# Expert weights loaded in 1 MB units with 8 KB rows, inputs gathered by every fourth column, and an overflow branch written as loops

## The chip, the core and the metric

One core of one Trainium2 chip. TensorE (PE) multiplies, VectorE (DVE), ScalarE (ACT) and GpSimd (POOL) do the rest, and SyncE (SP) issues all DMAs from one queue. The metric is the device time of one launch in microseconds (us). The kernel before took 753.24, 752.36 and 753.23 us in three runs, median 753.23 us.

## The reference

Two layers on 256 tokens of width 1024, all in float32. Each layer has a mixer (layer 0: sparse attention, layer 1: latent attention) beside a cross-attention, one output projection, a residual with layer norm, and a mixture of experts:

```
hdn = silu(einsum('sd,edf->sef', xs, w_gate)) * einsum('sd,edf->sef', xs, w_up)
hdn = hdn * gate[..., None]          # gate: top-1 group of 4, top-2 experts within it
f   = einsum('sef,efd->sd', hdn, w_down)
x   = layer_norm(ALPHA * x + f, ln_g, ln_b)
```

There are 16 experts of hidden width 512. Each of the three matrices of an expert is 1024 x 512 floats, 2 MB, so that the experts of a layer hold about 100 MB, and the two layers read nearly all of their bytes for them.

## The kernel before, in words

**The mixture of experts.** `moe` (L1459) works through eight pairs of experts, k = 0 to 7. Up to 64 tokens are taken for each expert. For a pair, `gather` (L1521, pairs 0 and 1) or `gather_two` (L1508, two pairs at once) multiplies the tokens x_tm, as the stationary operand, by a 0/1 matrix of the chosen tokens. The result is the pair's input, transposed: eight chunks of 128 model columns by 128 places. A layer has five such gathers of 32 matmul instructions each (a float32 matmul shows as two instructions): two for the pairs 0 and 1, one each for the pairs 2 and 3, 4 and 5, 6 and 7. `up` (L1553) then multiplies the chunks by the gate weights and again by the up weights, the result is transposed in four blocks (L1682), multiplied by the down weights (L1728, for the last pair L1749), and `combine` (L1567) adds it back to the tokens. All of it is in program order on PE.

**Chunks.** A unit of gate or up weights is 256 rows of a matrix, two to a partition: partition p holds the rows 2p and 2p+1, 4 KB that are contiguous in memory. So the c-th chunk of inputs must hold every second model column (`chunk`, L1484), and PE loads its stationary operand from x_tm with a step of two floats. In the first gather of a layer the gains of the layer norm are applied chunk by chunk, from a small tile `vcol2` that is laid out in the same way; it comes from `vwide`, transposed in `g_pe` (L1038).

**Loads.** `plan_pair` (L278) lists the units of a pair: 24 units of 512 KB. `pump` (L228) goes through one list of all loads of the kernel in order; each takes a free slot in an arena of the on-chip memory, or in spare rooms that are opened during the experts, and is issued on SP's queue. When there is no slot, it stops until `drop` has freed one. SP waits for the last reader of a slot, and for earlier loads: some eight are under way at a time. `up` waits for the two units of a step, multiplies two chunks, frees both units and pumps. The inputs of the pairs stand in two more slots of the arena, xg0 and xg1 (`grab`, L1477).

**The overflow branch.** An expert may have been chosen by more than 64 tokens. Then the rest is computed by `overflow` (L1579), at the end of each layer, with all experts by all tokens. It stands under `tc.If(flag > 0)` (L1591), and its body is unrolled: 16 experts by 4 blocks of the hidden width, with 16 float32 matmuls for gate, 16 for up and 4 for down in each. With the inputs given the branch isn't taken, and every engine jumps over its part of the body. After it come the layer norm of layer 0 and the latent attention (`mla`, L1802: statistics L836, norm L877 and L878, 12 matmuls that only keep PE busy, L472, transposes L903), or in layer 1 `finish` (L2003), which writes the output.

## Time and profile before

| what | us |
|---|---|
| median of three runs (752.36 to 753.24) | 753.23 |
| the execution that was profiled | 753.32 |
| its span, first to last instruction | 751.5 |

| engine | busy us | share of the span |
|---|---|---|
| PE, matmuls | 706.3 | 94% |
| PE, loads of stationary operands | 416.9 | 55% |
| DVE | 310.1 | 41% |
| ACT | 194.4 | 26% |
| POOL | 146.4 | 19% |

235.67 MB went through the DMA queues, a mean of 314 GB/s. PE's busy time counts matmuls as they are in the pipeline, with ends that are modelled, so it hides short waits. The experts of layer 0 run from about 199 to 418 us and those of layer 1 from about 525 to 737 us.

### The profile page before, as it was taken

What the parts mean: (1) busy time and instruction counts of PE and PEld (TensorE: products, weight loads), DVE (VectorE), ACT (ScalarE), POOL (GpSimd) and SP (SyncE); (2) the same over time, 40 slices, a digit from 0 to 9 for tenths busy, and PEclk for the clock granted to TensorE, in tenths of its full rate; (3) what the DMA queues carried; (4) which work ended last, traced back from release to release, by engine and by line L of the source; (5) the groups of instructions that cost most, each with busy time, mean ns of one, the idle gap of its engine ahead of it and who ended that gap; (6) DMA issues with size and microseconds to landing.
All of it is one profiled execution on the core that took longest, in us unless ns stands there. A gap on an engine that the chain in (4) does not pass through costs nothing. (4 is left out here: it accounts for less than half of the span.)

```text
span 751.5 us, 11046 instructions
## 1 busy us (share of the span) xinstructions
PE 706.3 (94%) x4119; PEld 416.9 (55%) x4119; DVE 310.1 (41%) x732; ACT 194.4 (26%) x478; POOL 146.4 (19%) x165
## 2 busy tenths in 40 slices
PE   6999989889999999999999699999999999999992
PEld 6988978667643535335324377777444435343341
DVE  3389588994641211121110547747412212121105
ACT  3342253553320211101101265543212001011010
POOL 6876536030210400000000252021302000000002
PEclk9999999998999999999999899999999999999996
DMA  9876673935788999999999896457989999999981
GB/s 306 251 223 180 214 282 119 346 92 168 282 334 320 408 345 408 410 408 408 408 410 377 301 386 211 160 197 270 346 320 409 409 408 410 409 409 408 410 322 59
DMA packets 88625, 235.67 MB, mean 314 GB/s; under 512 B 13356, under 2 KB 32879, under 8 KB 88559
## 3 DMA queue, kind: packets, MB, share of 16 engines
q1 hardware_dynamic: 88558, 234.83, 83.5%
q8 instruction: 36, 0.59, 0.3%
q14 instruction: 31, 0.25, 0.1%
HBM read 233.76 MB, written 1.05 MB: 312 GB/s over the span
## 5 line engine op out<-in xcount | busy, mean ns | idle before, releaser
L369 POOL TENSOR_TENSOR wl<-arena,wh 128x1024 fp32r<-128x1024 f32 (+3 forms) x36 | 83.2, 2334 | 35.8 <-PE s L643 10.4
L1673 DVE SCALAR_TENSOR_TENSOR arena<-arena,u 128x512 f32<-128x512 f32 x16 | 12.0, 748 | 186.5 <-PE u L1559 105.4
L1559 PE MATMUL u<-arena 128*64 128x512 f32 x332 | 82.6, 594 | 0.8 <-DMA arena<-in_moe_w_up_dram 0.7
L871 POOL TENSOR_TENSOR lnmv<-lnmv,mhalf 128x1 f32<-128x1 f32 x8 | 6.4, 801 | 378.0 <-DVE lnmv L870 377.7
L1559 PE MATMUL g<-arena 128*64 128x512 f32 x324 | 79.5, 594 | 0.2 <-DMA arena<-in_moe_w_gate_dram 0.2
L1728 PE MATMUL yb<-arena 128*64 128x512 f32 x316 | 76.6, 595 | 0.0
L1733 DVE TENSOR_TENSOR y<-yb,y 128x512 fp32r<-128x512 f32 x28 | 19.4, 692 | 85.7 <-ACT y L1732 85.3
L1559 PEld LDWEIGHTS u<-arena 128*64 128x64 f32 x332 | 26.0, 137 | 48.8 <-issue 42.0
L660 ACT ACTIVATE arena<-s,mx 128x128 f32<-128x128 f32 (+1 forms) x88 | 37.4, 435 | 55.5 <-DVE mx L654 53.0
L1559 PEld LDWEIGHTS g<-arena 128*64 128x64 f32 x324 | 24.8, 137 | 43.7 <-issue 40.4
L1728 PEld LDWEIGHTS yb<-arena 128*64 128x64 f32 x316 | 23.7, 137 | 39.8 <-issue 37.9
L1732 ACT CAST y<-yb 128x512 fp32r<-128x512 f32 x28 | 16.4, 585 | 94.2 <-PE yb L1728 94.2
L1570 PE MATMUL acc<-y,SkT 128*128 128x512 f32 (+1 forms) x136 | 38.6, 406 | 0.0
L1684 ACT COPY arena<-hT 128x256 f32<-128x256 f32 x16 | 6.0, 372 | 119.3 <-DVE arena L1684 119.3
L1671 ACT ACTIVATE arena<-g 128x512 f32<-128x512 f32 x16 | 9.6, 597 | 93.4 <-PE g L1559 93.3
L1559 PE MATMUL g<-split,arena 128*64 128x512 f32 x104 | 32.3, 592 | 0.2 <-DMA split<-in_moe_w_gate_dram 0.2
L1570 PEld LDWEIGHTS acc<-y,SkT 128*128 128x128 f32 x136 | 22.5, 188 | 15.9 <-issue 12.9
L1728 PE MATMUL yb<-split,arena 128*64 128x512 f32 x116 | 31.1, 596 | 0.0
L654 DVE TENSOR_REDUCE mx<-s 128x1 f32<-128x128 f32 (+1 forms) x88 | 27.0, 362 | 4.9 <-PE s L643 3.3
L1559 PE MATMUL u<-split,arena 128*64 128x512 f32 x100 | 28.6, 592 | 0.0
L683 PE MATMUL pT<-ident,arena 128*128 128x128 f32 x140 | 22.4, 290 | 4.5 <-DVE arena L673 2.1
L673 DVE TENSOR_SCALAR arena<-arena,sm 128x128 f32<-128x128 f32 (+1 forms) x48 | 26.2, 588 | 0.9
(409 smaller groups left out, 1283.5 us busy)
## 6 DMA issues: line engine op xcount, KB each, us to landing
arena<-in_moe_w_gate_dram SPq DMA_DIRECT2D x97, 512.0 KB, 10.2
arena<-in_moe_w_down_dram SPq DMA_DIRECT2D x93, 512.0 KB, 10.2
arena<-in_moe_w_up_dram SPq DMA_DIRECT2D x92, 512.0 KB, 10.2
split<-in_moe_w_down_dram SPq DMA_DIRECT2D x31, 512.0 KB, 10.2
split<-in_moe_w_gate_dram SPq DMA_DIRECT2D x26, 512.0 KB, 10.2
split<-in_moe_w_up_dram SPq DMA_DIRECT2D x25, 512.0 KB, 10.2
arena<-in_nsa_w_in_dram SPq DMA_DIRECT2D x7, 1024.0 KB, 7.5
arena<-in_w_out_dram SPq DMA_DIRECT2D x8, 512.0 KB, 11.9
```

Of the source, the lines that this page charges most:

```text
L369: lo[j].tensor_tensor(wl[:, c, :], t[:, c, :], wh[:, c, :].bitcast(F32), op=OP.subtract)
L654: V.tensor_reduce(self.mx[i][:, t:t + 1], v, axis=AX.X, op=OP.max, negate=True)
L660: SC.activation(self.p[i][:, a:a + n], self.sb[i][:, a:a + n], AF.Exp, bias=self.mx[i][:, t:t + 1], scale=1.0, accum_out=self.sm[i][:, t:t ...
L673: V.tensor_scalar(v, v, self.sm[i][:, t:t + 1], g, op0=OP.mult, op1=OP.mult)
L683: PE.transpose(pt[:, j * P:(j + 1) * P], self.p[i][:, a:a + P], ident)
L1559: PE.matmul(b_[e * 64:(e + 1) * 64, :], at[k][1](i * 2 + c)[:, e * 64:(e + 1) * 64], w_[e][:, c, :], start=(i + c == 0), stop=(i == 3 and ...
L1570: PE.matmul(acc[t][hf][:, a:b], SkT[k % 2][:, t * P:(t + 1) * P], yhl[hf][n][:, a:b], start=(k == 0 and n == 0), stop=(k == 7 and n == 1 a ...
L1671: SC.activation(h_sb, gp, AF.Silu)
L1673: V.scalar_tensor_tensor(h_sb, h_sb, gs[:, k % 2:k % 2 + 1], up_, op0=OP.mult, op1=OP.mult)
L1728: PE.matmul(yb[hf][e * 64:(e + 1) * 64, :], hT[:, c, e * 64:(e + 1) * 64], w_[e][:, 0, hf * 512:(hf + 1) * 512], start=(c == 0), stop=(c = ...
L1732: SC.copy(yhl[hf][0], yb[hf])
L1733: V.tensor_tensor(yhl[hf][1], yb[hf], yhl[hf][0].bitcast(F32), op=OP.subtract)
```

## The change

Five things change together.

1. Units of 1 MB: a unit of gate or up weights is now 512 rows, four to a partition (8 KB contiguous), one of down weights 256 rows of 1024, two to a partition (8 KB). A pair has 12 units. The down units of the last pair stay as they were. Slots are taken at multiples of 8 KB, or of 4 KB for what is at most 4 KB.
2. `chunk` takes every fourth column, so that PE's stationary operand is read with a step of four floats (16 bytes). `vwide`, `vcol2` and the transposes in `g_pe` follow. The four transposes of the hidden values read every second column, except in the last pair.
3. xg0 is allocated with the temporaries of the layer, xg1 beside the split of x; the one-unit room `slot` goes; the limits of the arena are 12.25 and 8.25 KB in place of 12.5, 8.5 and 8.5, 4.5 KB.
4. Two small tiles (`sv`, `gs`) move into a constant tile.
5. The body of the overflow branch has two loops on the chip, over 16 experts and 4 blocks, in place of 64 copies.

```
-            return slice(m // 2 * 256 + m % 2, (m // 2 + 1) * 256, 2)
+            return slice(m // 4 * 512 + m % 4, (m // 4 + 1) * 512, 4)
...
+        for nm, w in (("g", A["moe_w_gate"]), ("u", A["moe_w_up"])):
+            for q in range(2):
+                for e in range(2):
+                    plan("%s%d_%d_%d_%d" % (nm, l, k, q, e), [P, 4, FF],
+                         (None, w[l, 2 * k + e][q * 512:(q + 1) * 512, :].rearrange("(p c) f -> p c f", c=4)))
+        w = A["moe_w_down"]
+        if k < 7:
+            for q in range(2):
+                for e in range(2):
+                    plan("d%d_%d_%d_%d" % (l, k, q, e), [P, 2, D],
+                         (None, w[l, 2 * k + e][q * 256:(q + 1) * 256, :].rearrange("(p c) f -> p c f", c=2)))
+            return
...
         def up(k, nm, b_):
-            for i in range(4):
-                keys = ["%s%d_%d_%d_%d_%d" % (nm, l, k, i // 2, i % 2, e) for e in range(2)]
+            for i in range(2):
+                keys = ["%s%d_%d_%d_%d" % (nm, l, k, i, e) for e in range(2)]
                 w_ = [get(key) for key in keys]
-                for c in range(2):
+                for c in range(4):
                     for e in range(2):
-                        PE.matmul(b_[e * 64:(e + 1) * 64, :], at[k][1](i * 2 + c)[:, e * 64:(e + 1) * 64], w_[e][:, c, :],
-                                  start=(i + c == 0), stop=(i == 3 and c == 1))
+                        PE.matmul(b_[e * 64:(e + 1) * 64, :], at[k][1](i * 4 + c)[:, e * 64:(e + 1) * 64], w_[e][:, c, :],
+                                  start=(i + c == 0), stop=(i == 1 and c == 3))
...
-                for e in range(NE):
-                    for f in range(FF // P):
-                        fs = slice(f * P, (f + 1) * P)
+                with tc.For_i(0, NE, 1) as e:
+                    with tc.For_i(0, FF // P, 1) as f:
...
-                                V.scalar_tensor_tensor(z, yo, go[:, t, e:e + 1], z, op0=OP.mult, op1=OP.add)
+                                V.scalar_tensor_tensor(z, yo, go[:, t, 0:1], z, op0=OP.mult, op1=OP.add)
...
-                PE.transpose(b_[:, j * P:(j + 1) * P], h_sb[:, j * P:(j + 1) * P], ident)
+                PE.transpose(b_[:, j * P:(j + 1) * P], h_sb[:, j * P:(j + 1) * P] if k == 7 else
+                             h_sb[:, j // 2 * S + j % 2:(j // 2 + 1) * S:2], ident)
```

## Rows read from the trace of the kernel before

**Rows 1.** Stretches: length, busy PE, PEld, DVE, ACT, POOL, clock, DMA share, GB/s.
```profile
300.00:350.00 50.00, 50.00 (x247) 20.73 (x247) 8.56 (x17) 5.45 (x10) 0.00 (x0) 1.00 1.03 409
...
720.20:724.90 4.70, 4.70 (x25) 2.71 (x23) 1.17 (x2) 0.37 (x1) 0.00 (x0) 1.00 1.05 377
```

**Rows 2.** Timeline of PE, layer 0, pairs 6 and 7: start, length, instruction, count.
```profile
358.95 0.59 PE L1559 MATMUL g<-slot,arena 128*64 128x512 f32 x1
...
372.79 1.21 PE L1570 MATMUL acc<-y,SkT 128*128 128x512 f32 x4
...
382.44 2.74 PE L1559 MATMUL g<-split,arena 128*64 128x512 f32 x10
...
402.18 1.22 PE L1570 MATMUL acc<-y,SkT 128*128 128x512 f32 x4
```

**Rows 3.** Timeline of PE, layer 1, the last pair's gate, and the combine after its up.
```profile
708.38 2.31 PE L1559 MATMUL g<-arena 128*64 128x512 f32 x9
...
722.22 1.20 PE L1570 MATMUL acc<-y,SkT 128*128 128x512 f32 x4
```

**Rows 4.** Timeline of PE, the first gather, and the ends of a gather for two.
```profile
199.56 4.07 PE L1526 MATMUL xg<-arena,x_tm 128*128 128x128 f32 x32
...
297.06 0.28 PE L1515 MATMUL xg<-SkR,xh 128*128 128x256 f32 x1
...
300.78 0.28 PE L1515 MATMUL xg<-SkR,xl 128*128 128x256 f32 x1
```

**Rows 5.** Groups of PE's loads by form: count, busy us, mean ns, idle before.
```profile
L1515 PEld LDWEIGHTS xg<-SkR,xh 128*128 128x128 f32 x96 | 18.7, 195 | 1.8 <-ACT y L1732 1.6
L1526 PEld LDWEIGHTS xg<-arena,x_tm 128*128 128x128 f32 x128 | 15.6, 196 | 2.3 <-issue 1.6 <-DVE arena L1490 0.7
L1559 PEld LDWEIGHTS u<-arena 128*64 128x64 f32 x332 | 26.0, 137 | 48.8 <-issue 42.0 <-DMA arena<-in_moe_w_up_dram 5.9 <-DMA arena<-in_moe_w_down_dram 0.9
L1836 PEld LDWEIGHTS mi<-arena 128*128 128x128 f32 x16 | 2.9, 189 | 2.7 <-issue 1.9 <-ACT arena L1822 0.8
```

**Rows 6.** Groups of VectorE's reductions by form, same columns.
```profile
L654 DVE TENSOR_REDUCE mx<-s 128x1 f32<-128x256 f32 x52 | 20.6, 415 | 1.5 <-PE s L638 1.5
L654 DVE TENSOR_REDUCE mx<-s 128x1 f32<-128x128 f32 x36 | 10.3, 285 | 3.4 <-PE s L643 3.3
L848 DVE TENSOR_REDUCE arena<-arena 128x20 f32<-128x160 f32 x2 | 0.8, 421 | 0.0
L1401 DVE TENSOR_REDUCE y<-y 128x40 f32<-128x160 f32 x2 | 0.6, 320 | 0.1
```

**Rows 7.** Line 1591: sequencer instructions; ns min/median/max, first and last start.
```profile
L1591 ACTq COMPARE_BRANCH  x2: 45/48/50, 416.8 to 736.2; - x2
L1591 ACTq EVENT_SEMAPHORE  x2: 17/17/17, 417.2 to 736.6; - x2
L1591 DVEq COMPARE_BRANCH  x2: 63/68/72, 417.3 to 736.6; - x2
L1591 PEldq COMPARE_BRANCH  x2: 3386/4712/6037, 417.7 to 737.1; - x2
L1591 DVEq EVENT_SEMAPHORE  x2: 21/21/21, 423.1 to 739.5; - x2
```

**Rows 8.** Timeline around the branch, layer 0, then layer 1.
```profile
423.28 0.70 DVE L836 BATCH_NORM_STATS2 lnst<-acc 128x6 f32<-128x512 f32 x1 [5.62 <-DVEq L1591]
423.91 5.28 PE L472 MATMUL warm<-onesb 128*128 128x512 bf16 x12 [6.29 <-PEq L1591]
...
425.55 0.75 DVE L878 SCALAR_TENSOR_TENSOR x_tm<-x_tm,lnmv,arena 128x512 f32<-128x512 f32 x1 [0.46 <-POOL lnmv L871]
...
428.98 0.66 PE L903 MATMUL pt<-ident,x_tm 128*128 128x128 f32 x4
429.48 1.03 PE L472 MATMUL warm<-onesb 128*128 128x512 bf16 x4
...
739.65 0.70 DVE L836 BATCH_NORM_STATS2 lnst<-acc 128x6 f32<-128x512 f32 x1 [2.41 <-DVEq L1591]
```

## The prediction

> **What bounds the kernel now.** The first view is the table of stretches. In the middle of an expert stage PE is busy all of the time at full clock and the DMAs run at 409 GB/s [rows 1]; the two are nearly balanced, so the table can't say which of them sets the end. The timeline of PE can. In layer 0, pair 6 goes from its first gate matmul at 358.95 to its first combine at 372.79, in 13.84 us; pair 7 needs 19.74, from 382.44 to 402.18 [rows 2]. The 5.90 us between them are waits for weights: the groups of PE's loads put 5.9 us of idle time on up weights [rows 5]. So layer 0 becomes bound by the DMAs in its last pair and by PE before. In layer 1 the last pair takes 13.84 us again (708.38 to 722.22) [rows 3]: PE sets the pace to the end, and whatever is added to PE there is added to the time. The third view is the one line of the branch. In layer 0 PE's jump takes 6.04 us, VectorE's next instruction comes 5.8 us after its own compare, and in layer 1 it is 3.39 and 2.9 us [rows 7]; the normalization starts after it [rows 8].

> **Gathers by every fourth column: the term that decides.** A gather's PE time is now set by 32 instructions at 0.120 us ((300.78 - 297.06) / 31), 3.84 us [rows 4]. Its matmuls take some 0.107 us of that, an estimate for 256 columns from warming matmuls of 512, four of which take 1.03 us with the tail of the last, so some 0.21 each [rows 8]. The load of the stationary operand is hidden behind them as long as it is the shorter one. What does the load take? Contiguous, 64 columns show 137 ns and 128 columns 189, so 0.81 ns per column and 85 fixed; with a step of two floats the 128 columns show 195 and 196 [rows 5]. So a step of 8 bytes costs 6 ns, and no row has PE reading with a step of 16. The lower bound is that it costs as little again: pace 0.12, nothing. The upper bound comes from VectorE, which does read one float in 20. Its contiguous reductions take 285 ns for 128 elements and 415 for 256, 1.02 ns per element and 155 fixed, which gives 318 for 160 elements where 320 is shown; with a step of 80 bytes the same 160 take 421, or 1.66 ns each [rows 6]. If each newly fetched group of bytes takes 1.66 ns on PE too, the small rise at 8 bytes says how large the group is: with groups of 16 bytes the 128 columns are 64 fetches, 106 ns against 104 for the columns themselves, just over the edge; with 8 bytes it would be 212, which isn't seen, and with 32 bytes there would be no rise. At a step of 16 bytes each column is then a fetch: 128 x 1.66 = 212 ns, twice the matmul. I take this end, since it alone explains the rise, though the step of 8 bytes is the nearer row. The pace becomes 212 and a few ns, 0.22 us; a gather 7.04; five gathers of a layer cost 5 x 3.2 = 16.0 us more on PE. Between the two ends lies a load that adds VectorE's extra 0.64 ns to each column, 186 ns: pace 0.19, 11.2 us per layer.

> [...]

> In layer 1 the 16.0 us are on the path. In layer 0 they come before the last pair, whose waits of 5.90 they swallow: the weights land meanwhile. Layer 0 pays 16.0 - 5.9 = 10.1.

> **Larger units.** Two bounds from the stretches: rows of 4 KB at 409 GB/s are 160.2 ns on each of 16 engines; where rows of 2 KB flow, at 377, 86.9 [rows 1]. A row's fixed part is then 2 x 86.9 - 160.2 = 13.6 ns; an 8 KB row takes 306.8 and the rate is 427, 4.4% more. The other end is no gain, since a stretch that short may be poor in DMAs for another reason. Either way it is worth nothing where PE bounds. A step of `up` now waits for two units of 1 MB and then multiplies four chunks; the part that follows the last landing is two chunks longer, 2 x 13.84 / 16 = 1.7 us, which counts only where weights are late. SP issues half as many loads; PE's waits halve, hidden.

> **The branch.** ACT's body before is 64 activations, and its next instruction follows the compare by 0.4 us; VectorE's, with five vector operations in each of 64 copies, stalls 5.8, and PE's, with thousands, 6.0 [rows 7]. Short bodies are jumped without a stall. In loops, VectorE's body is some 25 operations and PE's some 180 records (16 transposes, 36 matmuls), the one below ACT's, the other between ACT's and VectorE's. I take both as free. In layer 0 VectorE's statistics then start 5.4 us earlier, and the first norm, which ends at 426.30, at 420.9. PE, now idle 6.29 us and then at half clock for 12 warming matmuls (5.28 us, where later four take 1.03), would do them in some 2.7 and be done at 420.9 also; the transposes, at 428.98 today, start at 421.2 [rows 8]: 7.8 us gained, and the attention behind them follows, its weights having been issued before the branch. In layer 1 only VectorE matters: it idles 2.41 us, of which 2.3 go [rows 8]. If PE's jump stays, layer 0 gains nothing, since its warming ends last already. The loops' own costs lie in the body that isn't run; if they put a barrier on the path beside it, that is at most the present stall again.

> **The rest.** Four more transposes at the start, and the limits of the arena, are hidden: 14 slots of 8 KB against 28 of 4 KB. The transposes of the hidden values read every second float: between nothing and the 6 ns that this step costs a gather's load [rows 5], 4 x 14 of them cost at most 0.3, which I take.

> **Sum, likeliest.** +10.1 (layer 0, gathers less waits) - 7.8 (its branch) + 16.0 (layer 1, gathers) - 2.3 (its branch) + 0.3 = +16.3. The profiled execution took 753.32, its span 751.5 and 1.8 around it; 753.3 + 16.3 = 769.6. The median of the runs is 753.23, 0.1 from the profiled one, so 769.6 stands for it too. With the load at 186 ns it is 753.3 + 5.3 - 7.8 + 11.2 - 2.3 + 0.3 = 760.0; the case's own range is 758 to 774.

> **Rival 1: every fourth column is free.** For it: the step of 8 bytes costs 6 ns, and VectorE needn't tell of PE. Then layer 0's waits shrink: 100 us of loads ahead of the last pair at 4.2% less are 4.2 us, less 1.7 for the longer last step, 2.5 gained. Layer 1 gains its branch alone. 753.3 - 2.5 - 7.8 - 2.3 + 0.3 = 741.0; 739 to 747, by the DMAs' rate. It decides if the load stays under 0.107.

> **Rival 2: PE's load slows by half of it** (a load of 145 to 165 ns). Layer 0 even, layer 1 +6: 753.3 + 0.5 - 7.8 + 6 - 2.3 + 0.3 = 750.0.

> **Rival 3: PE still stalls at the jump**, since its body lies between the two known lengths; layer 0's 7.8 are not gained. 777.4 with slow loads, 748.8 with free ones. [...]

> **Chances.** Likeliest case 0.48, rival 1 0.38, rival 2 0.07, rival 3 0.07. About 0.2% is what a measurement of this kernel can tell from no change. Slower: 0.48, and 0.05 of rivals 2 and 3, 0.53; same 0.04; faster 0.38 and 0.05, 0.43. Cases of both signs hold most of it, so the range has to span them: 740 leaves out a fifth of rival 1, 773 what of the stalls lies above.

> **What would show it.** The stationary loads of the gathers at 295 ns (85 + 212) where 195 stood, 0.22 us from one to the next and a gather of 7 us; the last pair of layer 0 in 13.8 us with no wait for weights; the compare on PE and VectorE under 0.1 us, and the statistics 0.4 us after it. Loads at 200 ns make the prediction wrong at its main term, and the time is then near 741.

## The result and the profile after

The changed kernel takes 773.0 us, median of four runs (772.74 to 774.40), against 753.24 before: a ratio of 1.0269 [1.0251, 1.0287], 19.8 us slower. That is the likeliest case of the prediction, but 3.4 us above its 769.6, and just above the upper end, 773, of its range: the two middle runs took 772.79 and 773.22. The profiled execution has a span of 771.1 us, 19.6 more than before, and the stretches below add up to that.

The groups of PE's stationary loads by form, of the changed kernel, answer to [rows 5] (count, busy us, mean ns, idle before):

```profile
L1513 PEld LDWEIGHTS xg<-SkR,xh 128*128 128x128 f32 x96 | 31.6, 329 | 1.8 <-ACT y L1733 1.6
L1524 PEld LDWEIGHTS xg<-arena,x_tm 128*128 128x128 f32 x128 | 30.3, 328 | 2.3 <-issue 1.6 <-DVE arena L1487 0.7
L1557 PEld LDWEIGHTS u<-arena 128*64 128x64 f32 x176 | 15.8, 137 | 25.1 <-issue 25.1
L1681 PEld LDWEIGHTS hT<-ident,arena 128*128 128x128 f32 x64 | 8.8, 202 | 3.3 <-DVE arena L1672 3.3
```

The loads of the gathers take 329 ns where 195 stood, and up's loads in this row no longer wait for weights. The timeline of PE shows the first gather, a gather for two pairs from its first to its last matmul, the last pair of layer 0 from gate to combine, and that of layer 1 ([rows 2 to 4] of before):

```profile
198.04 7.73 PE L1524 MATMUL xg<-arena,x_tm 128*128 128x128 f32 x32
...
306.81 0.28 PE L1513 MATMUL xg<-SkR,xh 128*128 128x256 f32 x1
...
313.93 0.39 PE L1513 MATMUL xg<-SkR,xl 128*128 128x256 f32 x1
...
399.46 0.59 PE L1557 MATMUL g<-split,arena 128*64 128x512 f32 x1
...
413.30 1.20 PE L1566 MATMUL acc<-y,SkT 128*128 128x512 f32 x4
...
730.76 3.60 PE L1557 MATMUL g<-arena 128*64 128x512 f32 x16
...
744.60 1.21 PE L1566 MATMUL acc<-y,SkT 128*128 128x512 f32 x4
```

From one gather matmul to the next it is now (313.93 - 306.81) / 31 = 0.230 us, where 0.120 stood. Both last pairs take 13.84 us, layer 0's too: its weights have landed while PE was held up in the gathers. The sequencers at the branch (now line 1587), and the timeline behind it in layer 0 and layer 1 ([rows 7, 8] of before):

```profile
L1587 DVEq COMPARE_BRANCH  x2: 56/64/72, 428.4 to 759.0; - x2
L1587 DVEq EVENT_SEMAPHORE  x2: 21/21/21, 428.8 to 759.7; - x2
L1587 PEldq COMPARE_BRANCH  x2: 318/338/358, 428.8 to 759.5; - x2
```

```profile
429.33 2.75 PE L475 MATMUL warm<-onesb 128*128 128x512 bf16 x12 [0.61 <-PEq L1587]
429.35 0.70 DVE L839 BATCH_NORM_STATS2 lnst<-acc 128x6 f32<-128x512 f32 x1 [0.58 <-PEq L1587]
...
432.52 0.63 PE L906 MATMUL pt<-ident,x_tm 128*128 128x128 f32 x4 [0.44 <-DVE x_tm L881]
...
759.85 0.70 DVE L839 BATCH_NORM_STATS2 lnst<-acc 128x6 f32<-128x512 f32 x1 [0.21 <-DVEq L1587]
```

PE's jump fell from 6.0 and 3.4 us to 0.36 and 0.32, VectorE's next instructions come 0.4 and 0.7 us after its compare, the 12 warming matmuls take 2.75 us where 5.28 stood (granted clock 1.00 in place of 0.50), and the transposes now wait for VectorE's norm, by 0.44 us.

Taking the same marks in both traces, the 19.6 us are: -1.5 before the first gather, +18.5 from it to the last pair of layer 0 (182.88 to 201.42), -5.9 in that pair, -7.6 at its branch (transposes 3.54 later, where the combine was 11.12 later), +0.1 to layer 1's first gather, +18.7 to its last pair (182.81 to 201.51), 0.0 in it, and -2.8 from the last matmul to the end.

The first of these isn't the change's. The table of stretches of the kernel before, and then of the changed one (length, busy PE, PEld, DVE, ACT, POOL, clock, DMA share, GB/s):

```profile
60.00:64.00 4.00, 4.00 (x22) 3.97 (x22) 3.43 (x12) 3.32 (x10) 0.00 (x0) 0.57 0.91 268
```

```profile
60.00:64.00 4.00, 4.00 (x35) 4.00 (x35) 3.43 (x12) 3.35 (x10) 0.00 (x0) 1.00 0.85 264
```

In both executions PE had been idle for most of the 2 us before (busy 0.69 and 0.73 us from 58 to 60); from 60 to 64 its granted clock was 0.57 in the one execution and 1.00 in the other. The lower clock comes and goes between executions: from 60 to 62 two kernels below were granted 0.50 (the units alone) and 1.00 (the loops alone), and another, profiled twice, starts its first gather at 199.40 and at 198.01.

### The profile page after: what moved, and what is told of

It reads as the page before. It is cut to its first block, busy times and chain, and to the rows that moved or that the text cites. A ratio compares the mean times of both kernels' runs of the same rounds, so it can differ in the third digit from the quotient of the medians.

```text
span 771.1 us, 10672 instructions
## 1 busy us (share of the span) xinstructions
PE 735.7 (95%) x4123; PEld 452.3 (59%) x4123; DVE 310.9 (40%) x732; ACT 194.5 (25%) x478; POOL 146.8 (19%) x165
## 5 line engine op out<-in xcount | busy, mean ns | idle before, releaser
L1729 PE MATMUL yb<-arena 128*64 128x512 f32 x328 | 85.3, 595 | 0.0
L1672 DVE SCALAR_TENSOR_TENSOR arena<-arena,csb,u 128x512 f32<-128x512 f32 x16 | 12.0, 747 | 180.9 <-PE u L1557 99.7
L1557 PE MATMUL g<-arena 128*64 128x512 f32 x200 | 53.8, 593 | 0.0
L1557 PE MATMUL u<-arena 128*64 128x512 f32 x176 | 50.4, 592 | 0.0
L1557 PE MATMUL u<-arena,xg 128*64 128x512 f32 x168 | 39.6, 592 | 0.0
L1557 PE MATMUL g<-arena,xg 128*64 128x512 f32 x144 | 39.6, 592 | 0.0
L1513 PE MATMUL xg<-SkR,xl 128*128 128x256 f32 x96 | 38.0, 396 | 0.0
L1513 PE MATMUL xg<-SkR,xh 128*128 128x256 f32 x96 | 37.8, 394 | 0.0
L1513 PEld LDWEIGHTS xg<-SkR,xh 128*128 128x128 f32 x96 | 31.6, 329 | 1.8 <-ACT y L1733 1.6
L1566 PEld LDWEIGHTS acc<-y,SkT 128*128 128x128 f32 x136 | 22.6, 189 | 15.9 <-issue 12.9
L1524 PEld LDWEIGHTS xg<-arena,x_tm 128*128 128x128 f32 x128 | 30.3, 328 | 2.3 <-issue 1.6
## 6 DMA issues: line engine op xcount, KB each, us to landing
split<-in_moe_w_gate_dram SPq DMA_DIRECT2D x13, 1024.0 KB, 12.5
```

The costliest lines, as they stand in the source:

```text
L1513: PE.matmul(b_[:, c * S:(c + 1) * S], v[:, t, chunk(2 * c0 + c)], SkR[:, t].rearrange("p e s -> p (e s)"), start=(c == 0 and t == 0 and v ...
L1524: PE.matmul(b_[:, c * P:(c + 1) * P], x_tm[:, t, chunk(c0 + c)], Sk[:, t].rearrange("p e s -> p (e s)"), start=(t == 0), stop=(t == 1))
L1557: PE.matmul(b_[e * 64:(e + 1) * 64, :], at[k][1](i * 4 + c)[:, e * 64:(e + 1) * 64], w_[e][:, c, :], start=(i + c == 0), stop=(i == 1 and ...
L1566: PE.matmul(acc[t][hf][:, a:b], SkT[k % 2][:, t * P:(t + 1) * P], yhl[hf][n][:, a:b], start=(k == 0 and n == 0), stop=(k == 7 and n == 1 a ...
L1672: V.scalar_tensor_tensor(h_sb, h_sb, gs[:, k % 2:k % 2 + 1], up_, op0=OP.mult, op1=OP.mult)
L1729: PE.matmul(yb[hf][e * 64:(e + 1) * 64, :], hT[:, 2 * q + c, e * 64:(e + 1) * 64], w_[e][:, c, hf * 512:(hf + 1) * 512], start=(q + c == 0 ...
```

## The experiments

**The two parts alone.** The first kernel keeps units and gathers of before and takes the loops; the second is the changed kernel with the branch unrolled again.

```diff
-                for e in range(NE):
-                    for f in range(FF // P):
+                with tc.For_i(0, NE, 1) as e:
+                    with tc.For_i(0, FF // P, 1) as f:
```

> The kernel before, with the body of the overflow branch alone written as loops on the chip; units and gathers stay as they were. Theory A (the two parts of the change are separate, the branch gives back what the trace shows): the jump costs PE some 0.35 us in place of 6.0 and 3.4, the first transposes of layer 0's normalization start 7.6 us earlier and VectorE's last statistics 2.2 us earlier, so 753.2 - 9.8 = 743.4 us, and all of it stays. Rival C (the earlier start is lost again, since layer 1's attention or experts then wait for weights that arrive no earlier): the stretch from the branch to the last pair of layer 1 grows by what the branch gave, 749 to 753 us. In both the gathers keep 0.12 us from one matmul to the next and the last pair of layer 0 its 5.9 us of waits.

> The changed kernel with the body of the branch unrolled again as before: the larger units and the gathers by every fourth column alone. Theory A: 773.0 + 9.8 = 782.8 us, PE's jump back at about 6 and 3.4 us. Rival C: the branch was worth little in the total and the units cost less than the gathers show, 773 to 777 us.

The loops alone: 742.80 against 751.96 of the kernel before on the same chip, ratio 0.9874 [0.9851, 0.9897], 9.2 us faster. The units alone: 784.75 (782.8 expected), ratio 1.0436 [1.0411, 1.0461], 32.8 us slower. The product of the two, 1.0305, is 0.4% above the 1.0269 of the whole change, no more than the intervals allow, so neither part needs the other. Theory A holds, and rival C falls: from the transposes behind the branch to layer 1's first gather the loops alone take 96.54 us and the kernel before 96.59, so what the branch gave isn't lost there. A little of it is lost later: layer 1's last pair now waits for weights and takes 14.29 us from gate to combine in place of 13.84. PE's jump in the units alone:

```profile
L1587 PEldq COMPARE_BRANCH  x2: 3326/4752/6177, 430.3 to 769.1; - x2
```

**Step or size.** One index of the changed kernel, and then one rearrangement of its weights (with the index of the gathers and the layout of the gains, which follow it):

```diff
-            return slice(m // 4 * 512 + m % 4, (m // 4 + 1) * 512, 4)
+            return slice(m * P, (m + 1) * P)
```

> The changed kernel with one index changed: the gathers read 128 neighbouring columns in place of every fourth (which leaves out the matching of the columns with the rows of the weights, so the values differ); units, transfers, waits and the number of instructions stay. Theory A (the step of 16 bytes alone makes the stationary load slow): loads of 189 ns, a gather of 3.7 us, and 753.2 - 9.8 for the branch, less 0.8 for layer 1's gathers without a step and 0 to 2.5 for the shorter waits in layer 0's last pair: 740 to 742.6 us. Rival B (the loads are slow because transfers of 8 KB rows write the on-chip memory beside them): loads stay near 329 ns and the time near 773 us.

```diff
-plan(..., [P, 4, FF], (None, w[...][q * 512:(q + 1) * 512, :].rearrange("(p c) f -> p c f", c=4)))
+plan(..., [P, 2, 2 * FF], (None, w[...][q * 512:(q + 1) * 512, :].rearrange("(b p c) f -> p b (c f)", b=2, c=2)))
-            return slice(m // 4 * 512 + m % 4, (m // 4 + 1) * 512, 4)
+            return slice(m // 2 * 256 + m % 2, (m // 2 + 1) * 256, 2)
```

> The changed kernel with the gate and up units still of 1 MB, but each as two rows of 4 KB per partition, so that the gathers read every second column again; the down units keep their 8 KB and the branch its loops. The result is the reference's. Theory A: gathers at 0.12 us again, and 1 MB units are worth nothing where PE bounds; layer 0's last pair waits about 5.9 us and up to 1.7 more for its longer last step: 743 to 745 us. Rival B (the size of the units is what slows the loads or the stages): over 755 us. If 8 KB rows of the down weights alone make the transfers faster, the waits of layer 0 fall and it is 741 to 743 us.

With neighbouring columns: 739.04, ratio 0.9823 [0.9801, 0.9846], 12.9 us faster than before. With 1 MB units and steps of two floats: 744.11, ratio 0.9897 [0.9877, 0.9917], and loads of 196 ns. The first one's loads, the same loads of the second, and the first one's rate in mid-stage:

```profile
L1513 PEld LDWEIGHTS xg<-SkR,xh 128*128 128x128 f32 x96 | 18.4, 191 | 1.8 <-ACT y L1733 1.6
L1557 PEld LDWEIGHTS u<-arena,xg 128*64 128x64 f32 x168 | 12.7, 137 | 24.7 <-issue 22.3 <-DMA arena<-in_moe_w_up_dram 2.4
```

```profile
L1513 PEld LDWEIGHTS xg<-SkR,xh 128*128 128x128 f32 x96 | 18.8, 196 | 1.8 <-ACT y L1733 1.6
```

```profile
300.00:350.00 50.00, 50.00 (x247) 20.96 (x244) 8.82 (x18) 5.26 (x10) 0.00 (x0) 1.00 1.01 419
```

In the first one the transfers of 8 KB rows and the instructions are the same, and the loads are back at 191 ns: the step alone makes them slow, and rival B falls. With PE that much faster, up waits for weights again (2.4 us in the row). This is the world of the prediction's first rival, and its 741.0 was near. The expectation's 740 to 742.6 was counted from 753.2 and is 1 us too high, about as much as the kernel before took less on this chip (751.96). The 8 KB rows give 419 GB/s where 409 stood [rows 1], and the waits of layer 0's last pair shrink: 17.04 us from gate to combine, 19.74 before.

**The price of a step.** Sets of 24 equal matmuls behind the end of the kernel before, one line each:

```diff
+    [PE.matmul(bb[:, 0:256], xa[:, 0:382:3], mv, start=True, stop=True) for _ in range(24)]
```

> The kernel before, with sets of 24 matmuls behind its end, which differ in one thing each: the step with which the stationary operand of 128 columns is read (1, 2, 3, 4, 6, 8, 12, 15 floats; 1, 2, 4, 6, 8, 16 values of 2 bytes), with 64 moving columns or 256; and, with a contiguous stationary operand, the step of 256 moving columns (1, 2, 3, 4, 7 floats). Only the rows of these sets count, not the time. Theory A (the load pays for each group of 16 bytes that it touches, 0.2335 us / 128 = 1.82 ns): 32, 64, 96, 128 groups at steps 1 to 4 and 128 beyond, so a load-bound pace of 0.107 at step 1 and 0.117, 0.175, 0.234 us at 2, 3, 4, and 0.234 at all larger steps; values of 2 bytes slow down by the step in bytes, 0.117 at 4 (8 bytes), 0.175 at 6 (12), 0.234 at 8 (16). Rival D (a threshold: every step of 16 bytes or more costs a column 1.82 ns, below it nothing): step 3 like step 2, about 0.107 to 0.117. Rival E (the cost grows with the step itself): step 8 near 0.47 us. Moving columns, if they are read in the same way: 256 of them 0.11 us at step 1, 0.35 at step 3, 0.47 at step 4 and 7.

The loads of the sets with 256 moving columns, at a granted clock of 1.00: steps of 1, 2, 3, 4 and 8 floats (ns min/median/max, first and last start):

```profile
L2057 PEld LDWEIGHTS bench<-SkR,xh x24: 188/192/224, 797.6 to 800.4; 128*128 128x128 f32 x24
L2058 PEld LDWEIGHTS bench<-SkR,xh x24: 195/195/198, 800.5 to 803.3; 128*128 128x128 f32 x24
L2059 PEld LDWEIGHTS bench<-SkR,xh x24: 251/261/261, 803.4 to 807.4; 128*128 128x128 f32 x24
L2060 PEld LDWEIGHTS bench<-SkR,xh x24: 317/329/332, 807.5 to 812.9; 128*128 128x128 f32 x24
L2061 PEld LDWEIGHTS bench<-SkR,xh x24: 337/337/341, 813.1 to 818.7; 128*128 128x128 f32 x24
```

From load to load that is 0.12, 0.12, 0.174, 0.235 and 0.243 us. Step 3 touches 96 groups of 16 bytes and step 4 128; 0.174 / 96 and 0.235 / 128 are both 1.8 ns. Rival D (step 3 like step 2) and rival E (step 8 twice step 4) fall: at steps of 3 and 4 these paces fit a load that pays 1.8 ns for each group of 16 bytes that it touches. The sets with 64 moving columns show the same in another light, since PE, which had a granted clock of 1.00 until 751 (the set of step 1), had 0.50 from 753 to 792. Steps 1, 3, 4, 6 and 12, and the table of a stretch of step 4:

```profile
L2043 PEld LDWEIGHTS bench<-SkR,xh x24: 190/192/192, 748.8 to 751.5; 128*128 128x128 f32 x24
L2045 PEld LDWEIGHTS bench<-SkR,xh x24: 329/329/331, 756.4 to 761.3; 128*128 128x128 f32 x24
L2046 PEld LDWEIGHTS bench<-SkR,xh x24: 329/329/331, 761.5 to 766.9; 128*128 128x128 f32 x24
L2047 PEld LDWEIGHTS bench<-SkR,xh x24: 316/318/319, 767.1 to 772.2; 128*128 128x128 f32 x24
L2049 PEld LDWEIGHTS bench<-SkR,xh x24: 364/369/369, 778.2 to 784.3; 128*128 128x128 f32 x24
```

```profile
761.60:766.90 5.30, 5.30 (x24) 5.30 (x25) 0.00 (x0) 0.00 (x0) 0.00 (x0) 0.50 0.00 0
```

At 1.00 the contiguous loads follow one another at (751.5 - 748.8) / 23 = 0.117 us. At 0.50 step 3 rises from 0.174 to (761.3 - 756.4) / 23 = 0.213 us, but step 4 takes the same 0.235 as at 1.00: its price did not rise with the lower clock. Beyond step 4 theory A's one price is only near: at 0.50 it is 0.222 us at step 6, 0.239 at 8, 0.265 at 12 and 0.230 at 15, so 1.7 to 2.1 ns a column. What sets these differences isn't shown. Its figures for moving columns and for values of 2 bytes were wrong; the last section has them.

**How long a body is jumped without a stall.** The kernel before, with 4, 8, 1 and 2 experts written out in the body of a loop:

```diff
+                with tc.For_i(0, NE // 4, 1) as eo:
+                    for j in range(4):
+                      for f in range(FF // P):
```

> The kernel before, with a middle length of the overflow branch: a loop over four groups of 4 experts, and inside it 4 experts written out. PE's body has 592 matmuls, 1184 records with their loads, where the loops have 52 matmuls and the full body 2320. [...] Rival G (the stall grows with the length that is jumped): a quarter of 6.0 and 3.4, so 1.5 and 0.9 us, and some 2 us in the time.

> The same with two groups of 8 experts: PE's body has 1168 matmuls, 2336 records. [...] Rival G: half, 3 and 1.7 us, 747. [...]

> The kernel before, with the overflow branch as one loop over the 16 experts whose four column blocks are written out: PE's body has 160 matmuls, 320 records with their loads; VectorE's some 35 operations. The runs so far show PE's jump at 0.34 us over 52 matmuls and at 3.3 to 6.1 us over 592, 1168 and 2320 alike, so the stall is no price per instruction but one that sets in between 104 and 1184 records. If it sets in above 320: compare 0.35 us and a time near 743. If below: 3.3 and 6.1 us and 749 to 751.

> The same with two experts written out: PE's body has 304 matmuls, 608 records. If the stall sets in above 608: 0.35 us and a time near 743. If below: 3.3 and 6.1 us and 749 to 751. A stall between the two (half of it) would speak for a price by length after all.

One execution each: 749.58, 753.38, 750.63 and 751.18 us, with 752.64 (the first two) and 751.44 (the others) for the kernel before beside them. PE's jump, with 1 and with 4 experts written out:

```profile
L1591 PEldq COMPARE_BRANCH  x2: 3426/4762/6097, 417.4 to 736.9; - x2
```

```profile
L1591 DVEq COMPARE_BRANCH  x2: 63/68/72, 416.8 to 735.8; - x2
L1591 PEldq COMPARE_BRANCH  x2: 3346/4712/6077, 417.2 to 736.3; - x2
L1591 DVEq EVENT_SEMAPHORE  x2: 21/21/21, 417.4 to 736.5; - x2
```

The stall hardly depends on the length: with 1, 2, 4, 8 and 16 experts written out it is 6.0 to 6.2 us in layer 0 and 3.3 to 3.4 in layer 1, but for 3.9 there with 8, and over the loops' body it is 0.34. So there is no price by length (rival G falls), and in these runs the stall sets in between the loops' body and that of one expert. The expectations put these at 104 and 320 records, with one matmul and one load for each matmul written. By the two instructions that a float32 matmul shows as they would be 176 (the prediction's "some 180") and 608. Where between the two it sets in, no run shows.

What ends the stall can be seen in the DMA queues. For the kernel before, the table of stretches from PE's compares on, in layer 0 and in layer 1, and the instruction queue q8 behind each (421.2 to 422.4, and 738.0 to 739.2; packets, MB, share):

```profile
417.70:421.20 3.50, 0.00 (x0) 0.00 (x0) 0.00 (x0) 0.00 (x0) 0.00 (x0) 1.00 1.03 404
737.10:738.10 1.00, 0.10 (x1) 0.00 (x0) 0.14 (x1) 0.00 (x0) 0.00 (x0) 1.00 0.06 16
```

```profile
q8 instruction: 1, 0.02, 5.6%
q8 instruction: 1, 0.02, 5.3%
```

One packet of q8 (some 16 KB: 0.59 MB in 36 packets over the span) starts 3.5 us after the compare in layer 0, and 1.0 in layer 1; each takes about 1 us, and PE goes on 1.4 us later. The run with one expert written out, which stalls twice as well, has 36 packets of q8 in its span too; the loops alone and the changed kernel have 34, and in the changed kernel none starts within the short jumps (428.8 to 429.2 and 759.5 to 759.9). The stall is thus, as far as a trace can tell, a fetch of instructions, and layer 0's, whose packet starts 2.5 us later, is 2.65 us longer. There the DMA engines are full with weights (share 1.03, against 0.06); that this is what holds the fetch up is not shown.

VectorE goes on 0.6 and 0.7 us after its compare over the body of four experts, 97 operations by the code (17 around the blocks, 5 in each of 16), and stalls over the 177 of eight: there its sequencer's next instruction starts at 423.0, behind a compare at 417.1. The run with four experts, in which PE alone stalls, also parts the gain: layer 0's transposes come 26.48 us after the combine of its last pair (26.80 before, 19.22 after the change), and the end 26.50 us after that of layer 1 (29.3 before, 26.50 after). So layer 0's gain hangs on PE's jump and layer 1's on VectorE's, as the prediction had it.

**The best of both.** 8 KB rows for the down weights alone, whose order the gathers don't share; gate and up in 512 KB and 4 KB rows, gathers by two, the branch in loops. It was timed twice, the second time on one chip with the loops alone:

> The changed kernel with gate and up units of 512 KB and 4 KB rows as before, gathers by every second column; the down units alone keep 1 MB and 8 KB rows (with the transposes of hidden values by every second float), and the branch its loops. Theory A: the transfers gain on a third of the bytes, some 2 us until layer 0's last pair, without its longer last step (the run with 1 MB units waits 1.7 us more there); layer 1 pays about 0.5 us for the strided transposes: 741 us, 1 to 3 us below the loops alone, the shortest of those that compute the reference. Rival H (8 KB rows gain only where all weights have them): 743 to 744 us.

> The loops alone once more, beside the kernel with 8 KB rows for the down weights alone, since the two were timed on different chips (9.2 and 13.1 us under the kernel before there). Their profiles differ by 1.7 us at the end of layer 0's up weights and by 0.5 in layer 1 the other way. By the traces: 742 to 743 us here and 1 to 2 us more than the other. If the difference of the first timings holds: 4 us more.

> The kernel with 8 KB rows for the down weights alone, 4 KB rows and steps of two floats for gate and up, and the loops, beside the loops alone. By the traces 1 to 2 us less than the loops alone, 740 to 741.5; if the difference of the first timings holds, 4 us less.

The mixed kernel: 739.55, ratio 0.9825 [0.9805, 0.9845]; again 739.36, 0.9828 [0.9815, 0.9842]. The loops alone beside it: 742.81, 0.9876 [0.9861, 0.9891]. So it is 3.4 us below the loops alone and rival H falls; it is some 13 below the kernel before and 33 below the changed one. In the spans of the second pair it is 2.1 us (740.7 to 738.6): the combine of layer 0's last pair comes at 399.10 in place of 400.77, and layer 1's last pair takes 13.84 us in place of 14.88, for with the branch's gain layer 1 had begun to wait for weights itself; the strided transposes take some of it back. The rest of the 3.4 lies between executions: the profiled one of the mixed kernel took 740.33, 1.0 above its median, and that of the loops alone 742.54, 0.3 below.

## What the prediction had right, and the step that failed

**The gathers** were the term that decides, and they went the way that was forecast: at a step of four floats the load takes 329 ns where 195 stood, the gather's pace rises from 0.120 to 0.230 us, and PE pays. That each column is then a fetch of its own is the prediction's estimate, and the sets above fit it. Its size was too small, and that is the step that failed. The fetch was priced at 1.66 ns from VectorE's reductions; on PE it is 1.8 (0.235 / 128). A gather cost 3.5 to 3.7 us more (the first one 7.66 from its start to the gate where 4.00 stood) and not 3.2, so a layer's pairs took 18.5 and 18.7 us more where 16.0 and the transposes' 0.15 were counted. These 5 us, less the 1.5 of the clock, are nearly the whole error; some 4 of them are the gathers'. The sentence that failed is thus "each newly fetched group of bytes takes 1.66 ns on PE too": right in kind, 10% low. With 16.0 us a layer the likeliest case had a range of its own up to 774, but the range that was given ended at 773. That VectorE's price came so near to PE's is luck, since no run shows why the two engines should pay the same. PE's own rows gave more: by the fixed 85 ns, (195 - 85) / 64 = 1.72 ns for each group. The groups of 16 bytes, read off 6 ns of difference between steps of one and two, fit what came: the set with step 3, which no row of before could show, fell on the line (0.174 / 96, 1.8 ns). The load was to show 295 ns and shows 329.

**Layer 0's waits** of 5.9 us were swallowed in full (13.84 for 19.74), as forecast. **The branch** gave 7.6 of the 7.8 us in layer 0 and 2.2 of 2.3 at VectorE's statistics in layer 1; rival 3 didn't come. PE's compare, which was to take under 0.1 us, took 0.32 and 0.36. That a short body is jumped without a stall was argued from ACT's 64 instructions. The series shows that PE's jump takes 0.34 us over the loops and 6.1 and 3.4 over one expert written out: nothing in the rows of before put the one below the stall and the other above it, and that the loops are below is in part luck. **The larger units** were to be worth nothing where PE bounds, and 1.7 us dearer where weights are late. The run with 1 MB units and 4 KB rows bears it out: it differs from the mixed kernel in the size of the gate and up units alone, and its layer 1 takes as long (183.40 us from the first gather to the last pair and 13.84 in it, against 183.35 and 13.84), while the last pair of its layer 0 takes 19.75 us, 2.0 more than the mixed kernel's 17.75, and layer 1's first gather starts 2.1 us later (516.98, 514.87). In the medians it is 744.1 against 739.4 us, on different chips; what more there is than 2 us the traces don't show. **The rate of 8 KB rows** was put at 427 GB/s and is 419. The stretch of the kernel before that was to show rows of 2 KB (720.20 to 724.90) held shorter rows as well, 347 of its 1087 packets being of 512 bytes to 2 KB, so a row's fixed part came out too high (by the 419 it would be 7.6 ns where 13.6 was taken, an estimate):

```profile
DMA packets 1087, 1.77 MB, mean 377 GB/s; under 512 B 55, under 2 KB 402, under 8 KB 1086
```

**The transposes** of the hidden values were put at 0.3 us in all; the runs with steps of two floats need 0.5 a layer more (182.88 to 183.34 in the mixed kernel), since their loads went from 142 ns to 199, and to 202 in the changed kernel. The prediction priced them by the gathers' 6 ns, but a contiguous load is shorter here, 142 ns in the row of the kernel before where the gathers' price was read off one of 189. By the price found above their 64 groups would take 85 + 64 x 1.8 = 200 ns, an estimate that uses the prediction's fixed part.

```profile
L1682 PEld LDWEIGHTS hT<-ident,arena 128*128 128x128 f32 x64 | 6.9, 142 | 3.3 <-DVE arena L1673 3.3
```

## What to carry to other kernels

A layout that lengthens the rows of a transfer can lengthen the step of an on-chip read elsewhere: count how often the reader uses each 16 bytes. A stationary load of 128 float32 columns cost 0.117 us without a step here, and 0.174 and 0.235 at steps of three and four; as an estimate from these, take the larger of the first figure and 1.8 ns for each 16 bytes touched. Where transfers were hidden, as in layer 1, their rate bought nothing (from its first gather to its last pair 183.35 us at 412 GB/s in the mixed kernel, 182.86 at 409 in the loops alone), and the strided read was paid in full (18.7 us more in the changed kernel); give the long rows to the operand whose order nobody else must follow, here the down weights. A branch that isn't taken still cost PE its jump, 0.32 and 0.36 us over the loops; what removed the stall was the body in loops, and not merely a shorter one, for over one expert written out it was 6.1 and 3.4 us, as over sixteen.

## What the runs showed of the hardware

**A moving operand paid in another way.** The sets with a contiguous stationary operand and 256 moving columns, at a granted clock of 1.00 and steps of 1, 2 and 4 floats:

```profile
L2062 PEld LDWEIGHTS bench<-xh x24: 188/192/208, 818.9 to 821.7; 128*128 128x128 f32 x24
L2063 PEld LDWEIGHTS bench<-xh x24: 192/208/208, 821.8 to 826.9; 128*128 128x128 f32 x24
L2065 PEld LDWEIGHTS bench<-xh x24: 207/209/209, 832.6 to 837.9; 128*128 128x128 f32 x24
```

**Values of 2 bytes paid about a quarter.** Loads of 128 such columns, once the granted clock was back at 1.00, at steps of 6, 8 and 16 values (12, 16 and 32 bytes):

```profile
L2054 PEld LDWEIGHTS <-xh x24: 132/144/145, 793.6 to 794.7; 128*128 128x128 bf16 x24
L2055 PEld LDWEIGHTS <-xh x24: 158/171/174, 794.7 to 796.1; 128*128 128x128 bf16 x24
L2056 PEld LDWEIGHTS <-xh x24: 172/173/175, 796.1 to 797.6; 128*128 128x128 bf16 x24
```

From load to load 0.048, 0.061 and 0.065 us, over 96, 128 and 128 groups, so about 0.5 ns for each 16 bytes touched, a quarter or so of the 1.8, where theory A had expected 0.175 us at 12 bytes and 0.234 at 16.
